# Where the low parts of the attention weights are computed: vector engine or GpSimd, in a three-branch attention kernel on Trainium2

## The chip, the cores and the metric

The kernel runs on one core of a Trainium2 chip, as one program and one launch. The metric is device microseconds from start to end. A core has five engines with queues of their own: TensorE (PE, with its weight loads listed apart as PEld), VectorE (DVE), ScalarE (ACT), GpSimd (POOL) and SyncE (SP), which here only issues DMAs. Each engine takes its instructions strictly in the order of its queue; waits between engines are semaphores.

## The reference

One layer of a hybrid decoder on a sequence of 512 rows with 1024 channels, all in float32. The input is RMS-normed and projected by one large matrix; three attention branches (A: block-sparse with blocks of 256; B: three dilated windows with dilation 1, 4 and 16; C: a sliding window of 128 with sinks) work on heads of 64; their outputs are gated, projected and merged. Cut to what matters:

```python
hn = rms_norm(x, ln_g[l])
proj = jnp.einsum('bsd,dc->bsc', hn, w_in[l])
(qa, ka, va, ga, qb, kb, vb, gb, qc, kc, vc, gc, gate_logits) = jnp.split(proj, SPLIT_POINTS, axis=-1)
...   # q and k of every head are RMS-normed: rms_norm(q.reshape(b, s, H, HEAD_DIM), g)
o_a = moba_attention(qa, ka, va, rel_bias_a)
o_b = dilated_attention(qb, kb, vb, rel_bias_b)
o_c = swa_sink_attention(qc, kc, vc, sinks[l], rel_bias_c)
branches = jnp.stack([o_a * jax.nn.silu(ga), o_b * jax.nn.silu(gb), o_c * jax.nn.silu(gc)], axis=2)
br = jnp.einsum('bsiw,iwd->bsid', branches, w_branch[l])
merged = jnp.sum(jax.nn.sigmoid(gate_logits) * br, axis=2)
x = x + jnp.einsum('bsd,de->bse', merged, w_out[l])
```

## The kernel before

**Split operands.** TensorE multiplies in the type fp32r, so every float32 operand is split in two: a high part `hi` (the value rounded to fp32r, a cast) and a low part `lo = value - hi` (a subtraction). A product is three matmuls: hi by hi, hi by lo, lo by hi. The weights come by DMA in tiles `w32` of 128x1024 floats (four buffers). For each, ScalarE casts `whi` (`split_hi`, L132), and one of two engines subtracts to get `wlo` (`split_lo`, L137); `whi` and `wlo` have six buffers each. The subtraction reads two operands from SBUF and writes one to SBUF.

**Who subtracts.** `load_w` (L148 to L167) counts the weight tiles of the whole kernel in `nw`. On L164 the tiles whose number is divisible by `every` go to GpSimd, the rest to the vector engine. The default of `every` is `LOEVERY`, 4 before the change. The very first call has `early=True` and alternates. The loads of the branch projections and of the output projection pass `every=1000`; the faster gate blocks have a loader of their own (`fast_weights`) whose subtractions are on the vector engine. None of these change.

**Stages.** The attention is done in ten units: A0, W0, R0, Z0, A1, W1, R1, Z1, C0, C1 (W, R and Z are branch B with dilation 1, 4 and 16; the digit is the half of the heads). A unit's weights are six tiles: four for q and k, two for v (C0 has four in all, C1 two). First a unit is projected (L492, L493 and L494 are the three matmuls, in four row blocks t = 0 to 3). For q and k each row block goes through a chain: ScalarE copies the result to `qn` (L504) and squares it (L506); the vector engine sums (`ss`, L508) and adds the epsilon (`rv`, L141); **GpSimd takes the power -1/2 (`rr`, L143)**; the vector engine multiplies (`qn`, L519); TensorE transposes (`tr`, L549); ScalarE and the vector engine make the high and low parts `qhi`, `khi`, `qlo`, `klo` (L559, L560). So `rr` and the weight subtractions of GpSimd share one queue. Then the unit's attention runs: scores on TensorE (`sc`; L652, L750), minimum and sum on the vector engine (L576), the exponential on ScalarE (L577), transposes (L672, L761), `pthi` on ScalarE and `ptlo` on the vector engine (L132 and L137 with other operands), and the weighted values (L565 to L567, L602). In a window of the code the projection matmuls of the next unit are put between the steps of this one's attention, to keep TensorE busy. After every Z unit branch B is merged: statistics are transposed (`trs` L953), permuted by three copies on ScalarE (`un`, L957) and transposed back (`trb`, L960).

After C1 come the raw gate columns and, from about 480 us on, the gate blocks and projections. Jobs 0, 1 and 2 (raw B, raw A and the first gate block) are loaded with `load_w`; these are what the code calls `n < PLAIN`.

**Order.** The engines' order is not written out by hand. The program is built in a context that schedules with a model of the times (`schedule_with_timeline_sim=True`), so when an instruction changes its engine, the order on all engines is worked out anew.

Of the kernel before, what the change touches and what calls it, by code (L numbers as in the profile page):

```python
# [20 lines left out]
KT = 8  # L21
# [7 lines left out]
UNITS = ("A0", "W0", "R0", "Z0", "A1", "W1", "R1", "Z1", "C0", "C1")  # L29
SPILL = [(k, h) for k in "ABC" for h in range(2) if UNITS.index(("Z" if k == "B" else k) + str(h)) < len(UNITS) - KEEP]  # L30
ORDER = "BAC"
LOEVERY = 4


RATION = {"A0": (52, 0.65), "W0": (52, 0.65), "W1": (52, 0.65), "C0": (8, 0.6), "C1": (0, 0.9)}
# [65 lines left out]
def body(tc, x, ln_g, w_in, qk_g, sinks, w_branch, w_out, rel_bias, c_ident, c_onehot, c_mask, c_expand, out):  # L101
# [9 lines left out]
    with top:  # L111
# [18 lines left out]
        def split_hi(dst, src, eng=A):  # L130
            if eng is A:
                A.copy(dst, src)  # L132
            else:
                eng.tensor_copy(dst, src)  # L134

        def split_lo(dst, src, hi, eng=V):
            eng.tensor_tensor(dst, src, hi.bitcast(F32), ALU.subtract)  # L137
# [9 lines left out]

        def load_w(pieces, kts, early=False, every=LOEVERY):  # L148


            ncol = sum(n for n, _ in pieces)
            per = 1024 // ncol
            his, los = [], []
            for k0 in range(0, kts, per):
                w = wp.tile([128, per, ncol], F32, name="w32", tag="w32", bufs=LBUFS)
                o = 0
                for n, src in pieces:
                    nc.sync.dma_start(w[:, :, o : o + n], src(k0, k0 + per))
                    o += n
                hi = wp.tile([128, per, ncol], F32R, name="whi", tag="whi")  # L160
                lo = wp.tile([128, per, ncol], F32R, name="wlo", tag="wlo")
                nw[0] += 1
                split_hi(hi, w, V if early and nw[0] % 2 else A)
                split_lo(lo, w, hi, G if nw[0] % (2 if early else every) == 0 else V)  # L164
                his.append(hi)
                los.append(lo)
            return (lambda k: his[k // per][:, k % per]), (lambda k: los[k // per][:, k % per])  # L167

        def win_piece(c, n):
            return (n, lambda k0, k1: win[:, k0:k1, c : c + n])  # L170
# [106 lines left out]
        def fast_weights(src):  # L277

            L = {}
            for i, k in ((0, 0), (1, 0), (1, 1), (0, 1)):
                L[i, k] = wp.tile([128, 4, 256], F32, name="w32", tag="w32", bufs=LBUFS)
                nc.sync.dma_start(L[i, k], src(i, k))
            sets = []

            def parts(w, eng):
                hi = wp.tile([128, 4, 256], F32R, name="whi", tag="whi")
                lo = wp.tile([128, 4, 256], F32R, name="wlo", tag="wlo")
                split_hi(hi, w)  # L290
                split_lo(lo, w, hi, eng)
                sets.append((hi, lo))

            sm = gp.tile([128, 4, 256], F32, name="sm", tag="sm", bufs=1)
            parts(L[0, 0], V)
            V.tensor_tensor(sm, L[1, 0], L[1, 1], ALU.add)
            parts(sm, V)
            V.tensor_tensor(sm, sm, L[0, 0], ALU.subtract)
            parts(sm, V)
            parts(L[0, 1], V)  # L300
            V.tensor_tensor(L[0, 0], L[0, 0], L[1, 0], ALU.subtract)
            parts(L[0, 0], V)
            parts(L[1, 1], V)
            V.tensor_tensor(sm, L[0, 1], sm, ALU.subtract)
            parts(sm, V)
            return sets
# [97 lines left out]
        def job_load(n):  # L404
            if n >= len(jobs):
                return None
            ty, u, v = jobs[n]
            if ty in ("raw", "gl"):
                c0 = v if ty == "raw" else GL + v * D + u * 512
                if n < PLAIN:  # L410
                    return load_w([win_piece(c0, 512)], KT)
                return fast_weights(lambda i, k: win[:, 4 * k : 4 * k + 4, c0 + 256 * i : c0 + 256 * i + 256])
            if ty == "br":
                return load_w([(512, lambda k0, k1: wbr[v, :, k0:k1, u * 512 : u * 512 + 512])], 4, every=1000)
            return load_w([(1024, lambda k0, k1: wou[:, k0:k1, :])], KT, every=1000)
# [7 lines left out]
        def raw_columns():  # L423
            jw[0] = job_load(0)
            for n in range(2):
                br = jobs[n][1]
                jw[n + 1] = job_load(n + 1)
                for hf in range(2):
                    raw = raw_tile(br, hf)
                    for p in range(2):  # L430
                        pj = ps.tile([128, 512], F32, name="pj", tag="pj")
                        yield from gate_cols(jw[n], (hf * 2 + p) * 128, pj)
                        A.copy(raw[:, p], pj)
# [598 lines left out]
        for n in range(2, len(jobs) - 1):  # L1032
            ty, dh, i = jobs[n]
            if n == PLAIN:
                xs = fast_x()
            w, wnext = wnext, job_load(n + 1)
            if ty == "raw":
                fast_cols(w, xs, [raw_tile(dh, hf) for hf in range(2)], keep)
# [92 lines left out]
```

## Time and profile before

| | |
|---|---|
| median of three runs | 805.29 us (805.21 to 806.34) |
| the profiled execution | 808.76 us |
| its span, first to last instruction | 807.0 us |
| TensorE busy | 783.0 us, 97% |
| vector engine busy | 515.6 us, 64% |
| ScalarE busy | 432.4 us, 54% |
| GpSimd busy | 128.2 us, 16% |
| mean granted TensorE clock | 0.987 of full |

The span is 1.76 us shorter than its execution's time. The profiled execution is 3.5 us longer than the median of the runs. Times of rows below are microseconds from the start of the span. "x2" in a row of the timeline means two instructions in a row, with their total time; the bracket is the engine's idle time before, and what ended it.

### The profile page before, as it was taken

How to read it: one execution, taken by the hardware profiler on the slowest of the kernel's cores; microseconds unless marked ns; L12 is line 12 of the kernel's file. 1: busy time of each engine (PE TensorE's matmuls, PEld its weight loads, DVE VectorE, ACT ScalarE, POOL GpSimd, SP SyncE). 2: the span in 40 equal slices, each digit the busy share in tenths (PEclk: the TensorE clock that was granted, in tenths of full speed). 3: DMA queues.
4: the chain of work that ended last, by engine and by line, in shares of the span. 5: the costliest groups of instructions: out<-in, count | busy, mean ns of one | idle time of the engine just before them, and what ended most of it. 6: DMA issues, size and time to landing. Idle time of an engine off the chain costs nothing.

```text
span 807.0 us, 12636 instructions
## 1 busy us (share of the span) xinstructions
PE 783.0 (97%) x4727; PEld 663.4 (82%) x4727; DVE 515.6 (64%) x1088; ACT 432.4 (54%) x938; POOL 128.2 (16%) x90
## 2 busy tenths in 40 slices
PE   7999999999998999999999899999999999999997
PEld 4887887788878777878887787788899999999886
DVE  6765664564554667346554486848889887987512
ACT  5534564666577356447775865766355244445300
POOL 5422211112310340122032042100000000000000
PEclk9999999999998999999999699999999999999999
DMA  9443343351331153414431221414143334436302
GB/s 280 126 150 85 103 121 102 106 168 35 105 111 27 52 157 79 142 46 147 131 105 33 80 65 42 154 54 137 46 157 123 90 102 131 131 101 201 117 1 104
DMA packets 67328, 85.72 MB, mean 106 GB/s; under 512 B 4899, under 2 KB 53155, under 8 KB 67268
## 3 DMA queue, kind: packets, MB, share of 16 engines
q1 hardware_dynamic: 67268, 84.93, 34.2%
q8 instruction: 37, 0.61, 0.3%
q14 instruction: 23, 0.19, 0.1%
HBM read 75.41 MB, written 9.50 MB: 105 GB/s over the span
## 4 chain that ended last, share of the span: by engine, by line
PE 88%; DVE 4%; ACT 4%; issue 2%; DMA 1%; POOL 0%; SPq 0%; DVEq 0%; ACTq 0%; POOLq 0%
PE pj L492 13%; PE pj L493 12%; PE pj L494 12%; PE fc L352 10%; PE acc L1090 5%; PE fsc L352 4%; PE po L602 3%; PE sc L652 3%; PE pj L272 2%; PE pj L274 2%; PE pj L273 2%; PE po L1060 2%; PE po L1061 2%; PE po L1062 2%; PE tr L672 2%; PE tr L549 2%
## 5 line engine op out<-in xcount | busy, mean ns | idle before, releaser
L492 PE MATMUL pj<-whi,xhi 128*128 128x512 f32 (+1 forms) x576 | 203.9, 354 | 2.0 <-DVE whi L134 0.9
L493 PE MATMUL pj<-wlo,xhi 128*128 128x512 f32 (+1 forms) x576 | 199.2, 346 | 0.0
L494 PE MATMUL pj<-whi,xlo 128*128 128x512 f32 (+1 forms) x576 | 198.1, 345 | 0.0
L132 ACT CAST whi<-w 128x1024 fp32r<-128x1024 f32 x108 | 112.8, 1050 | 77.5 <-PE fsc L352 18.7
L137 DVE TENSOR_TENSOR wlo<-w,whi 128x1024 fp32r<-128x1024 f32 x93 | 117.6, 1273 | 39.1 <-ACT whi L132 38.4
L492 PEld LDWEIGHTS pj<-whi,xhi 128*128 128x128 f32 x576 | 111.0, 193 | 18.6 <-ACT xhi L132 1.7
L493 PEld LDWEIGHTS pj<-wlo,xhi 128*128 128x128 f32 x576 | 111.1, 193 | 12.4 <-issue 0.8
L494 PEld LDWEIGHTS pj<-whi,xlo 128*128 128x128 f32 x576 | 111.0, 193 | 12.4 <-issue 0.5
L143 POOL TENSOR_TENSOR rr<-rv,mhalf 128x8 f32<-128x8 f32 (+2 forms) x40 | 65.7, 1644 | 218.3 <-DVE rv L141 199.0
L137 DVE TENSOR_TENSOR ptlo<-tr,pthi 128x128 fp32r<-128x128 f32 (+3 forms) x112 | 50.9, 458 | 30.6 <-ACT pthi L132 22.4
L132 ACT CAST pthi<-tr 128x128 fp32r<-128x128 f32 (+3 forms) x112 | 44.4, 400 | 39.9 <-PE tr L672 19.5
L137 POOL TENSOR_TENSOR wlo<-w,whi 128x1024 fp32r<-128x1024 f32 x17 | 41.1, 2419 | 98.5 <-ACT whi L132 98.5
L519 DVE TENSOR_TENSOR qn<-qn,rr 128x512 f32<-128x512 f32 (+1 forms) x36 | 30.9, 858 | 32.9 <-POOL rr L143 32.8
L576 DVE CUSTOM_DVE_ANT_0 lg<-sc,bt 128x128 f32<-128x128 f32 (+2 forms) x96 | 28.5, 335 | 24.6 <-PE sc L652 12.2
L508 DVE TENSOR_REDUCE ss<-sq 128x8 f32<-128x512 f32 (+2 forms) x40 | 25.7, 642 | 28.8 <-ACT sq L506 28.4
L577 ACT ACTIVATE lg<-lg,sm 128x128 f32<-128x128 f32 (+1 forms) x80 | 32.8, 411 | 14.0 <-DVE sm L576 13.7
L352 PE MATMUL fc<-xlo,whi 128*128 128x256 f32 x144 | 40.2, 279 | 0.0
L352 PE MATMUL fc<-xhi,wlo 128*128 128x256 f32 x144 | 40.2, 279 | 0.0
L352 PE MATMUL fc<-xhi,whi 128*128 128x256 f32 x144 | 40.2, 279 | 0.0
L272 PE MATMUL pj<-xhi,whi 128*128 128x512 f32 x96 | 39.2, 408 | 0.0
L504 ACT COPY qn<-pj 128x512 f32<-128x512 f32 (+1 forms) x36 | 20.6, 571 | 33.3 <-PE pj L494 33.3
L273 PE MATMUL pj<-xlo,whi 128*128 128x512 f32 x96 | 37.9, 395 | 0.0
(259 smaller groups left out, 1752.7 us busy)
## 6 DMA issues: line engine op xcount, KB each, us to landing
w<-in_w_in SPq DMA_DIRECT2D x54, 512.0 KB, 4.2
w<-in_w_in SPq DMA_DIRECT2D x72, 256.0 KB, 3.8
w<-in_w_branch SPq DMA_DIRECT2D x12, 512.0 KB, 3.5
vscr<-vn SPq DMA_DIRECT2D x16, 256.0 KB, 2.8
w<-in_w_out SPq DMA_DIRECT2D x8, 512.0 KB, 4.6
osp<-oraw SPq DMA_DIRECT2D x6, 512.0 KB, 4.2
oback<-osp SPq DMA_DIRECT2D x6, 512.0 KB, 3.6
xt<-in_x SPq DMA_DIRECT2D x4, 512.0 KB, 6.6
```

Of the source, the lines that this page charges most:

```text
L132: A.copy(dst, src)
L137: eng.tensor_tensor(dst, src, hi.bitcast(F32), ALU.subtract)
L143: G.tensor_tensor(r, v, mhalf[:, :n], ALU.pow)
L272: T.matmul(psum, a, xhi[:, k, :], start=(k == 0), stop=False)
L273: T.matmul(psum, a, xlo[:, k, :], start=False, stop=False)
L352: T.matmul(psum[:, c], w[:, k, cs], x_[:, k, :], start=(first and c == 0 and k == 0 and q == 0), stop=(c == 1 and k == 3 and q == 2), skip ...
L492: T.matmul(pj[:, :ncol], xh, whi(k), start=(k == 0), stop=False)
L493: T.matmul(pj[:, :ncol], xh, wlo(k), start=False, stop=False)
L494: T.matmul(pj[:, :ncol], xl, whi(k), start=False, stop=(k == KT - 1))
L519: V.tensor_tensor(q3[:, :nq], q3[:, :nq], r[:, :nq].unsqueeze(2).broadcast_to([128, nq, 64]), ALU.mult)
L577: last_exp[0] = A.activation(lg, lg, AF.Exp, bias=mcol, scale=-1.0, accum_out=lcol)
L1090: T.matmul(acc[t * 2 + e], part[k // 2][:, k % 2, tsl], wo[q](k)[:, es], start=(k == 0 and q == 0 and part is mhi), stop=(k == KT - 1 and ...
```

## The change

Two edits. `LOEVERY` goes from 4 to 1, so that all weight tiles loaded with the default go to GpSimd: in the attention all but two of the four tiles of the early call. And the three gate jobs loaded with `load_w` now pass `every=2`, so every second of their 12 tiles goes to GpSimd (before: every fourth).

```diff
-LOEVERY = 4
+LOEVERY = 1
...
                 if n < PLAIN:
-                    return load_w([win_piece(c0, 512)], KT)
+                    return load_w([win_piece(c0, 512)], KT, every=2)
```

Counted in the program, 41 of the 93 subtractions `wlo<-w32,whi` of the vector engine move: GpSimd has 58 of them after the change and 17 before, the vector engine 52 and 93. No other instruction is added or removed, but the schedule is worked out anew. In the rows below a number behind a name is that of the tile, the same in both programs.

**The end of unit Z1, vector engine.** Here (the rows at 440 to 446 us) the weight tiles 5108 to 5126 of raw B are split, between the softmax steps of the last Z unit. Before:

```order
L576 ISA sm_3443 128x1
L137 TENSOR_TENSOR wlo_5108<-w32_5105,whi_5107 128x1024
L137 TENSOR_TENSOR wlo_5120<-w32_5117,whi_5119 128x1024
L137 TENSOR_TENSOR wlo_5126<-w32_5123,whi_5125 128x1024
L576 ISA lg_4530,sm_3443<-sc_4517,bt_4518 128x128
L576 ISA sm_3443 128x1
L576 ISA lg_4530,sm_3443<-sc_4517,bt_4518 128x128
L576 ISA sm_3443 128x1
L137 TENSOR_TENSOR ptlo_98<-tr_4476,pthi_97 128x512
```

After:

```order
L516 TENSOR_TENSOR qn_4761<-qn_4761,rr6_4769 128x64 x2
L137 TENSOR_TENSOR wlo_5108<-w32_5105,whi_5107 128x1024
L137 TENSOR_TENSOR wlo_5120<-w32_5117,whi_5119 128x1024
L576 ISA lg_4530,sm_3443<-sc_4517,bt_4518 128x128
L576 ISA sm_3443 128x1
L576 ISA lg_4530,sm_3443<-sc_4517,bt_4518 128x128
L576 ISA sm_3443 128x1
L137 TENSOR_TENSOR ptlo_98<-tr_4476,pthi_97 128x512
```

One subtraction, wlo_5126, has left the queue ahead of `ptlo`; wlo_5120 is still there. On GpSimd wlo_5126 now stands directly behind wlo_5114.

**The end of unit Z0, vector engine.** Here stand the third row block's `qn` of unit A1 (with `rr8_2626`), eight softmax steps of Z0, and weight tiles of W1 (q and k). Before:

```order
L576 ISA lg_2305,sm_1253<-sc_2276,bt_2279 128x128
L576 ISA sm_1253 128x1
L519 TENSOR_TENSOR qn_2618<-qn_2618,rr8_2626 128x512
L137 TENSOR_TENSOR wlo_2805<-w32_2801,whi_2804 128x1024
L137 TENSOR_TENSOR wlo_2819<-w32_2815,whi_2818 128x1024
L137 TENSOR_TENSOR wlo_2826<-w32_2822,whi_2825 128x1024
L576 ISA lg_2352,sm_1253<-sc_2339,bt_2340 128x128
```

After:

```order
L508 TENSOR_REDUCE ss_2622<-sq_2620 128x8
L141 TENSOR_SCALAR rv8_2624<-ss_2622 128x8
L519 TENSOR_TENSOR qn_2618<-qn_2618,rr8_2626 128x512
L576 ISA lg_2289,sm_1253<-sc_2276,bt_2277 128x128
L576 ISA sm_1253 128x1
L576 ISA lg_2289,sm_1253<-sc_2276,bt_2277 128x128
L576 ISA sm_1253 128x1
L576 ISA lg_2289,sm_1253<-sc_2276,bt_2279 128x128
```

The three subtractions have left. `qn_2618` stood behind the eight softmax steps and stands ahead of them now.

**The merge of branch B after Z0, TensorE.** The transposes `trs_2402` feed the copies `un_2407` of ScalarE, for which `trb_2411` waits. Before:

```order
L953 MATMUL trs_2402<-idr_63,sl_1251 96x128 x4
L549 MATMUL tr_2542<-idr_63,qn_2526 128x128 x2
L494 MATMUL pj_2714<-whi_2271,xlo_65 128x256
L549 MATMUL tr_2583<-idr_63,qn_2572 128x128 x2
L492 MATMUL pj_2714<-whi_2271,xhi_64 128x256
L493 MATMUL pj_2714<-wlo_2272,xhi_64 128x256
L494 MATMUL pj_2714<-whi_2271,xlo_65 128x256
L960 MATMUL trb_2411<-idr_63,un_2407 128x96 x4
```

After, the last rows ahead of `trb_2411`:

```order
L494 MATMUL pj_2772<-whi_2265,xlo_65 128x256
L492 MATMUL pj_2772<-whi_2265,xhi_64 128x256
L493 MATMUL pj_2772<-wlo_2266,xhi_64 128x256
L494 MATMUL pj_2772<-whi_2265,xlo_65 128x256
L492 MATMUL pj_2772<-whi_2271,xhi_64 128x256
L493 MATMUL pj_2772<-wlo_2272,xhi_64 128x256
L494 MATMUL pj_2772<-whi_2271,xlo_65 128x256
L960 MATMUL trb_2411<-idr_63,un_2407 128x96 x4
```

Between `trs_2402` and `trb_2411` there were 4 projection matmuls and two pairs of transposes; now there are 39 projection matmuls and two such pairs.

**The projection of W0, GpSimd.** The powers are those of W0's last three row blocks, the weight tiles 1196 to 1230 are R0's. Before:

```order
L143 TENSOR_TENSOR rr8_739<-rv8_737,mhalf_67 128x8
L137 TENSOR_TENSOR wlo_1216<-w32_1212,whi_1215 128x1024
L143 TENSOR_TENSOR rr8_785<-rv8_783,mhalf_67 128x8
L143 TENSOR_TENSOR rr8_831<-rv8_829,mhalf_67 128x8
L810 MEMSET sl_2842 128x384
```

After:

```order
L143 TENSOR_TENSOR rr8_785<-rv8_783,mhalf_67 128x8
L137 TENSOR_TENSOR wlo_1196<-w32_1193,whi_1195 128x1024
L137 TENSOR_TENSOR wlo_1202<-w32_1199,whi_1201 128x1024
L137 TENSOR_TENSOR wlo_1209<-w32_1205,whi_1208 128x1024
L137 TENSOR_TENSOR wlo_1216<-w32_1212,whi_1215 128x1024
L143 TENSOR_TENSOR rr8_831<-rv8_829,mhalf_67 128x8
```

Four subtractions in a row now stand between the powers of the third and of the fourth row block, where there were none; the one before `rr8_785` has gone behind it. The same pattern, four subtractions in a row between a unit's third power and its fourth, stands in GpSimd's queue after the change in the chains of A0, R0, Z0, A1, R1 and Z1 too: seven times in all.

## Rows read from the trace of the kernel before

**Rows 1.** Page, part 1: busy us (share of the span) and instructions of each engine.

```profile
PE 783.0 (97%) x4727; PEld 663.4 (82%) x4727; DVE 515.6 (64%) x1088; ACT 432.4 (54%) x938; POOL 128.2 (16%) x90
```

**Rows 2.** Page, part 4: the chain that ended last, by engine.

```profile
PE 88%; DVE 4%; ACT 4%; issue 2%; DMA 1%; POOL 0%; SPq 0%; DVEq 0%; ACTq 0%; POOLq 0%
```

**Rows 3.** Page, part 5: groups, busy us, mean ns | idle before, releaser.

```profile
L137 DVE TENSOR_TENSOR wlo<-w,whi 128x1024 fp32r<-128x1024 f32 x93 | 117.6, 1273 | 39.1 <-ACT whi L132 38.4
...
L137 POOL TENSOR_TENSOR wlo<-w,whi 128x1024 fp32r<-128x1024 f32 x17 | 41.1, 2419 | 98.5 <-ACT whi L132 98.5
L519 DVE TENSOR_TENSOR qn<-qn,rr 128x512 f32<-128x512 f32 (+1 forms) x36 | 30.9, 858 | 32.9 <-POOL rr L143 32.8
```

**Rows 4.** Waits of PE: engine, line, waited for: us in total, times, longest.

```profile
PE po L566 <- DVE ptlo L137: 3.3, 5, 2.1
PE trb L960 <- ACT un L957: 2.7, 1, 2.7
...
PE tr L549 <- DVE qlo L560: 0.8, 2, 0.4
...
PE tr L672 <- DVE qlo L560: 0.7, 1, 0.7
PE tr L549 <- DVE klo L560: 0.6, 1, 0.6
```

**Rows 5.** Windows: length, busy us by engine, granted clock (PEclk), DMA share, GB/s.

```profile
252.90:256.20 3.30, 3.30 (x18) 3.30 (x17) 1.27 (x5) 3.16 (x5) 1.64 (x1) 0.50 0.26 76
447.40:461.00 13.60, 12.48 (x56) 10.67 (x55) 3.81 (x11) 12.87 (x32) 0.00 (x0) 0.50 0.20 78
```

**Rows 6.** Timeline, end of unit Z1: start, us, engine, operation, [idle <-releaser].

```profile
440.86 2.37 POOL L137 TENSOR_TENSOR wlo<-w,whi 128x1024 fp32r<-128x1024 f32 x1 [7.41 <-ACT whi L132]
441.76 3.69 DVE L137 TENSOR_TENSOR wlo<-w,whi 128x1024 fp32r<-128x1024 f32 x2 [1.83 <-ACT whi L132]
...
445.79 0.68 DVE L137 TENSOR_TENSOR ptlo<-tr,pthi 128x512 fp32r<-128x512 f32 x1
...
446.52 0.39 PE L566 MATMUL po<-ptlo,vhi 128*128 128x256 f32 x1 [2.12 <-DVE ptlo L137]
```

**Rows 7.** Timeline, end of unit Z0 and the merge of branch B.

```profile
227.03 0.69 DVE L519 TENSOR_TENSOR qn<-qn,rr 128x512 f32<-128x512 f32 x1
227.64 1.22 DVE L137 TENSOR_TENSOR wlo<-w,whi 128x1024 fp32r<-128x1024 f32 x1
231.57 3.67 DVE L137 TENSOR_TENSOR wlo<-w,whi 128x1024 fp32r<-128x1024 f32 x2 [2.71 <-ACT whi L132]
...
240.20 0.33 PE L761 MATMUL tr<-idr,lg 128*128 128x128 f32 x1 [0.82 <-ACT lg L577]
...
251.24 0.55 PE L960 MATMUL trb<-idr,un 96*128 96x96 f32 x4 [2.67 <-ACT un L957]
```

**Rows 8.** Timeline: vector-engine instructions beside a subtraction of GpSimd, two places.

```profile
80.70 2.20 DVE L141 TENSOR_SCALAR rv<-ss 128x8 f32<-128x8 f32 x1
...
413.64 2.41 POOL L137 TENSOR_TENSOR wlo<-w,whi 128x1024 fp32r<-128x1024 f32 x1
...
413.71 2.89 DVE L519 TENSOR_TENSOR qn<-qn,rr 128x512 f32<-128x512 f32 x1 [0.39 <-POOL rr L143]
```

**Rows 9.** Timeline, projection of W0: the last two powers and what follows.

```profile
83.04 3.24 POOL L143 TENSOR_TENSOR rr<-rv,mhalf 128x8 f32<-128x8 f32 x2 [0.17 <-DVE rv L141]
...
86.31 0.69 DVE L519 TENSOR_TENSOR qn<-qn,rr 128x512 f32<-128x512 f32 x1 [0.21 <-POOL rr L143]
...
89.35 0.83 PE L549 MATMUL tr<-idr,qn 128*128 128x128 f32 x4 [0.40 <-DVE qlo L560]
```

**Rows 10.** Timeline, attention of A1 with the projection of W1 (317 to 319 us).

```profile
317.18 1.21 DVE L137 TENSOR_TENSOR wlo<-w,whi 128x1024 fp32r<-128x1024 f32 x1
...
318.83 0.44 PE L549 MATMUL tr<-idr,qn 128*128 128x128 f32 x2 [0.35 <-DVE qlo L560]
```

**Rows 11.** Timeline, projection of Z1, last row block: its power and its transpose.

```profile
420.13 1.64 POOL L143 TENSOR_TENSOR rr<-rv,mhalf 128x8 f32<-128x8 f32 x1 [4.08 <-DVE rv L141]
...
427.08 0.38 PE L549 MATMUL tr<-idr,qn 128*128 128x128 f32 x2
```

**Rows 12.** Page, part 6: DMA issues, count, KB each, us to landing.

```profile
w<-in_w_in SPq DMA_DIRECT2D x72, 256.0 KB, 3.8
```

## The prediction

> **What bounds the kernel now.** I read the busy shares first: TensorE is busy for 783.0 of 807.0 us, the vector engine for 515.6, GpSimd for 128.2 [rows 1]. The chain of work that ended last is TensorE for 88%, vector engine 4%, ScalarE 4%, GpSimd 0% [rows 2]. So a faster vector engine saves time only where TensorE stands and waits for it. TensorE's idle time is 807.0 - 783.0 = 24 us, and the list of its waits says for whom: 3.3 us for `ptlo`, 2.7 for the copies `un`, and a row of waits of 0.6 to 0.8 each for `qlo` and `klo` [rows 4]. To this come stretches with the granted clock at 0.50, which is 1.2 GHz. They follow such waits: 252.9 to 256.2 us behind the wait for `un`, and 447.4 to 461.0 behind the wait of 2.1 us for `ptlo` [rows 5 to 7]. A matmul of the first stretch takes 3.30 / 17 = 0.19 to 0.21 us where the full clock takes about half, so the two stretches cost at most 1.7 and 6.8 us. What the change can gain lies in these waits and stretches, not in the 50 us that it takes off the vector engine.
>
> **What moves.** 41 subtractions leave the vector engine, at 1.22 us where nothing disturbs them (mean 1.273): 41 x 1.22 = 50 us. GpSimd takes 2.419 us for one [rows 3], so it gains 41 x 2.42 = 99 us, 128 to 227, still 28% of the span. Both totals lie beside TensorE's work. If all of the difference of 1.15 us lay on the path, it would be +47 us; it doesn't, since the chain that ended last has nothing of GpSimd. What counts is where a burst of them stands ahead of something TensorE needs.
>
> The Trainium skill speaks against the move: its GPSIMD Engine Reference, section 4.1 (Engine selection), sends elementwise work with two inputs to VectorE and calls GpSimd about twice as slow. The trace agrees, 2419 to 1273 ns. By that rule alone the sum would be the +47 us; it holds for an engine whose time counts, which GpSimd's here is not.
>
> **What GpSimd's subtraction does to the vector engine.** The trace shows a second cost. A vector instruction whose operands all lie in SBUF, issued while GpSimd subtracts, ends only behind it: L519 at 413.71 took 2.89 us, beside a subtraction of GpSimd from 413.64 for 2.41, where others take 0.69; a tiny `rv` took 2.20 [rows 8]. The subtractions of the vector engine itself are held too: the pair at 441.76 took 3.69 where 2 x 1.22 = 2.44 is usual, beside GpSimd's from 440.86 to 443.23 [rows 6], and the pair at 231.57 took 3.67 [rows 7]. So each L519 or `rv` that meets a burst loses some 2.0 to 2.2 us. The held subtractions become fewer, the held L519 and `rv` more.
>
> **Part by part.** Times are those of the rows of before.
>
> *End of Z1.* wlo_5126, the second of the pair at 441.76, leaves the queue ahead of `ptlo` at 445.79, for which TensorE waited 2.12 us until 446.52 [rows 6]. wlo_5120 stays, and stays held. `ptlo` comes 1.2 us sooner, other inputs allowing: **-1.1**. If two subtractions of GpSimd in a row hold the vector engine for both, it is up to +2.4 - 1.2 = +1.2 instead. No row shows two in a row; I take the gain, since in both held pairs the vector engine went on as soon as the first one ended.
>
> *End of Z0 and the merge.* The wait of 2.67 us before `trb` at 251.24 [rows 7] has 35 more projection matmuls ahead of it, of about 0.12 us each: 35 x 0.12 = 4.2 us of cover, more than the wait, so it goes, less a rest: **-2.4**. With it may go the stretch at half clock: **-1.7**. These matmuls stood elsewhere before, so TensorE has less to do ahead of them. There, `qn_2618` now stands before the eight softmax steps instead of behind them, and it can meet wlo_2805 on GpSimd, which follows `rr8_2626` directly: a hold of 2.2 us on the softmax, whose results TensorE already waited for (0.82 at 240.20). Three subtractions that stood at 227.64 and 231.57, 1.22 + 3.67 = 4.9 us, are no longer in the way of the next softmax steps. I take **+1.7** for waits that grow there, between -1.5 (nothing is held; the 4.9 us help) and +4 (two holds). Sum of the place: -2.4, between -5.6 and +1.6.
>
> *Attention of A1 and like places.* The subtraction at 317.18 is followed by `qlo`, for which TensorE waited 0.35 us at 318.83 and then ran a slower transpose, 0.44 [rows 10]: it leaves, **-0.5**. Of the other waits for `qlo` and `klo`, 0.8 + 0.7 + 0.6 in all [rows 4] with this one inside, some go with it: **-0.5**, between 0 and -1.5.
>
> *The powers behind bursts.* Seven times four subtractions, 4 x 2.42 = 9.7 us, stand between the third `rr` of a unit and the fourth. In W0's projection the two powers ended at 83.04 + 3.24 = 86.28, L519 followed at 86.31, and TensorE's transpose came at 89.35, behind a short wait for `qlo` [rows 9]. After the change the burst starts behind the third power. That came as late as 83.04 because its `rv` was held [rows 8] behind subtractions that leave; I put its end between 76.5 and 79.2, an estimate from the row block's copy that feeds it. Then the burst ends between 86.2 and 88.9, the fourth power 1.64 later, L519 0.69 later, at 88.5 to 91.2; TensorE reached the transpose at 89.35 - 0.40 = 88.95. That is a wait of 0 to 2.3 us: **+1.1**. In Z1's projection the fourth power stood at 420.13 to 421.77 and its transpose at 427.08 [rows 11]; four subtractions behind the third power, which ended about 413.7 (GpSimd's next starts at 413.64 [rows 8]), end at 423.3, so the power slips by some 4 us and its L519 ends at 426.4: 0.7 us to spare. A1's chain is alike. A0's I put at +0.3. For those three **+0.8**, between 0 and +3. For the other three units I take nothing: their chains have what two holds cost, by the same counting, to spare.
>
> *Loads and buffers.* A weight tile's buffer is read until its subtraction ends, 1.2 us later than before and more within a burst. A tile lands 3.8 us after issue [rows 12], and the tiles are loaded a unit ahead: nothing; up to +1 if the SyncE queue stands behind one at a stage's start.
>
> *The first gate block.* Six instead of three of the 12 tiles on GpSimd; in Z1's end they are counted above. Behind 480 us there is nothing of GpSimd to collide with: nothing.
>
> **Sum.** -1.1 - 2.4 - 0.5 - 0.5 + 1.1 + 0.8 = -2.6 us. Against the profiled execution, 808.76, it is 806.2; that execution was 3.5 us above the median 805.29, so for the median I say **802.7**. Since the whole order is worked out anew, each place can move by some tenths in either direction; with the bounds above the forecast's own range is 798 to 806.
>
> **Rivals.**
> 1. *The bursts hold the chains* (slower). An `rv` or L519 of the fourth row block comes while the burst runs and is held 2.0 to 2.2 us, and the power behind it is late by 4 us already. Where 0.7 us are to spare a second hold shows as 1.3 to 1.5 us on TensorE, where nothing is to spare as 2.0. It decides from the point where L519 ends behind TensorE's reaching the transpose. Four of the seven bursts at 2.0: 802.7 + 8.0 = 810.7; two: 806.7. For it: rows 8 and 11. Against: the four subtractions are not always ready in a row, as each waits for its cast on ScalarE (98.5 us of GpSimd's idle time were spent so [rows 3]). Beside it, the GPSIMD Engine Reference of the Trainium skill, section 1 (Specifications), says that GpSimd shares its SBUF interfaces with VectorE and contends with its instructions that have two SBUF inputs; by that rule L519 and the low parts are held, and the trace agrees for L519, 2.89 for 0.69 us.
> 2. *Nothing in sum* (the same). TensorE is busy for 97%, the waits that go come back in other places as the same matmuls fill them: 805.3 +- 1.6.
> 3. *The long stretch at half clock goes as well* (faster). If the wait at the end of Z1 falls from 2.1 to about 1 us and the clock doesn't fall behind it, up to 6.8 us [rows 5] come back: 802.7 - 6.8 = 795.9. Against: ScalarE was busy 12.87 of these 13.6 us and TensorE waited there in many short pieces, which stay.
>
> That the change does nothing of what it says is excluded by the order: 41 subtractions stand on the other engine.
>
> **How the numbers follow.** A difference of 0.2%, 1.6 us, is about what a measurement of this kernel can tell. Forecast 0.42 (all faster); rival 3 0.12; rival 2 0.20; rival 1 0.26. So faster 0.54, same 0.20, slower 0.26. The range, 796.0 to 810.0, reaches to the middle of rival 1 and to rival 3 and leaves out some 0.1 at each end.
>
> **What would show it.** Right: the vector engine's busy time falls by 40 to 55 us and GpSimd's rises by about 99; TensorE's wait for `un` near 250 us is under 0.5; its wait for `ptlo` near 446 is about 1; L519 rows of 2.4 to 2.9 us become more than the few of now, but few are followed by a wait of TensorE at L549. Wrong: TensorE's waits at L549 or for L519's results of 1 to 2 us at the ends of projections (rival 1); the sum of TensorE's idle time unchanged at 24 us (rival 2); a stretch at half clock that is gone, or a new one (rival 3). My forecast falls if the reordering moved waits to places that I didn't go through, or if the vector engine is held for a whole burst.

## The result, and the profile after

The changed kernel takes 800.55 us (median of 4 runs, 799.89 to 801.07), the kernel before 805.82 beside it (4 runs, 805.21 to 807.13): a ratio of 0.9940, 95% interval 0.9927 to 0.9954. That is faster by 0.6%, or 5.3 us. Run once more, with e9 to e11, it was 0.9939 (0.9926 to 0.9953). The forecast was 2.6 us, to 802.7.

The profiled execution has a span of 799.3 us, 7.7 less than that of before. Busy shares and groups of the changed kernel:

```profile
PE 776.3 (97%) x4727; PEld 657.8 (82%) x4727; DVE 476.6 (60%) x1047; ACT 433.9 (54%) x938; POOL 224.1 (28%) x131
...
L137 POOL TENSOR_TENSOR wlo<-w,whi 128x1024 fp32r<-128x1024 f32 x58 | 140.7, 2442 | 113.8 <-ACT whi L132 99.9
...
L137 DVE TENSOR_TENSOR wlo<-w,whi 128x1024 fp32r<-128x1024 f32 x52 | 66.1, 1280 | 20.9 <-ACT whi L132 20.8
...
L519 DVE TENSOR_TENSOR qn<-qn,rr 128x512 f32<-128x512 f32 (+1 forms) x36 | 35.8, 996 | 23.2 <-POOL rr L143 23.0
```

Beside [rows 1, 3] the vector engine is busy 39.0 us less, GpSimd 95.9 us more. The mean of L519 went from 858 to 996 ns: more of them are held, which means that they have to wait for a subtraction of GpSimd to end. Waits of TensorE of the changed kernel:

```profile
PE po L566 <- DVE ptlo L137: 2.0, 4, 1.0
PE tr L761 <- ACT lg L577: 1.8, 3, 1.1
...
PE tr L549 <- DVE klo L560: 1.1, 1, 1.1
PE tr L672 <- DVE qlo L560: 0.9, 1, 0.9
PE tr L672 <- ACT lg L577: 0.8, 1, 0.8
PE tr L549 <- DVE qn L519: 0.7, 1, 0.7
```

The wait for `un` of [rows 4] is gone; that for `ptlo` fell from 3.3 to 2.0; waits for `lg` at L672 and for L519's result are new, that for `lg` at L761 is longer (0.8 before). TensorE's idle time fell only from 24.0 to 23.0 us. The rest of the profiled gain, 6.7 us, is in its busy time, of which a part is the clock. Span and mean granted clock of before, and then of the changed kernel:

```profile
core 0: 807.0 us, clock 0.987
...
core 0: 799.3 us, clock 0.991
```

A microsecond at the lower level, 1.2 GHz (a granted clock of 0.50), loses half at most, and (1 - 0.987) x 807 = 10.5 us, (1 - 0.991) x 799 = 7.2 us: up to 3.3 us of the 7.7 in this pair of executions are clock. The gain of the medians is not: when the two were run once more, the executions of the changed kernel had mean clocks of 0.991 to 0.995, those of the kernel before 0.992 to 0.996.

**Where the time went, by stage.** Instructions stand in another order in the two programs, so I lined them up by TensorE's work: every matmul of the program's order is given its pace (0.233 us for 512 columns, 0.117 for 256, 0.109 for 128; half for the scores' pairs), these are added up, and the trace tells when each sum was reached. The table gives the change against before in us, by stretches of before. Columns are single profiled executions, the changed kernel twice (ch, again), then the experiments by number (below; e5, which does more work, is left out). The execution of before is 3 us above its median, so gains look that much larger here; those of e6, e7, e8 and e9 were the fastest of their runs.

```
before, us        ch  again    e1    e2    e3    e4    e6    e7    e8    e9   e10   e11
  4.2- 32.8      1.1   -0.7   0.0  -0.3  -0.7  -1.5  -1.7  -1.2  -1.9  -0.5  -2.0   0.0
 32.8-142.9     -1.2   -0.3   0.1  -0.4   0.2  -2.2  -0.1  -1.4  -1.2  -1.5  -1.2  -1.3
142.9-168.0     -1.9   -1.9  -1.9   0.0  -0.5  -0.3   0.0  -1.9  -1.9  -1.9   0.0  -1.9
210.8-263.5     -3.2   -4.4  -2.8  -0.4  -1.8  -0.3  -3.2  -1.9  -4.4  -4.9   0.0  -2.9
263.5-354.5      0.3    0.3   0.3   0.1  -0.8   0.2  -1.1   0.2  -0.5   3.1  -0.1  -0.5
354.5-379.1     -2.0   -2.0  -2.0   0.0  -0.5   0.0   0.0  -2.0  -1.9  -2.0   0.0  -2.0
422.0-446.9     -1.1   -1.1   0.1  -1.1  -1.2  -1.1   0.0  -1.1  -1.1  -1.1   0.0  -1.1
446.9-474.3     -1.3   -1.2  -1.1   0.1  -1.8   0.2  -1.8  -1.4  -1.9  -1.3  -2.0  -1.4
474.3-580.0      1.7    1.7   1.2   2.3   0.2  -0.9  -0.4   0.3   0.4   1.7   1.2  -0.9
```

The stretches left out change by under 0.5, and behind 580 us nothing changes. The first row moves by 2 us even between two executions of the same kernel; the rows with -1.9, -2.0 and -1.1 repeat to a tenth.

Some of the other rows move with the clock. This is the time that each execution spent at 1.2 GHz in three of the stretches, the first column being the kernel before:

```
us at 1.2 GHz  before    ch  again    e1    e2    e3    e4    e6    e7    e8    e9   e10   e11
210.8-263.5       6.8   3.4    0.0   3.4   6.8   6.8   6.8   3.4   6.8   0.0   0.0   6.8   3.4
446.9-474.3      13.6   6.8    6.8   6.8  10.2   0.0  10.2   3.4   3.4   0.0   3.4   3.4   3.4
474.3-580.0       0.0   3.4    3.4   3.4   3.4   0.0   0.0   0.0   0.0   0.0   3.4   3.4   0.0
```

At half a microsecond for each, up to 1.7 us of the changed kernel's -3.2 at the end of Z0 and up to 3.4 of the second execution's -4.4 are clock. Without this, all columns lie between -1.0 and -1.9 there, but for e2, e4 and e10 with 0 to -0.4. Behind 474 us the columns with a stretch at 1.2 GHz have +1.2 to +2.3, the others -0.9 to +0.4. Between 446.9 and 474.3 us, 10 to 14 us less at 1.2 GHz are worth only 1.3 to 2.0 us. In the rows with -1.9, -2.0 and -1.1 no execution was at 1.2 GHz.

### The profile page after: what moved, and what is told of

Same layout as the page of the kernel before. It is cut to its first block, busy times and chain, and to the rows that moved or that the text cites. A ratio compares the mean times of both kernels' runs of the same rounds, so it can differ in the third digit from the quotient of the medians.

```text
span 799.3 us, 12655 instructions
## 1 busy us (share of the span) xinstructions
PE 776.3 (97%) x4727; PEld 657.8 (82%) x4727; DVE 476.6 (60%) x1047; ACT 433.9 (54%) x938; POOL 224.1 (28%) x131
## 4 chain that ended last, share of the span: by engine, by line
PE 85%; ACT 5%; DVE 3%; DMA 2%; POOL 2%; issue 2%; SPq 0%; DVEq 0%; ACTq 0%; POOLq 0%
PE pj L492 11%; PE pj L494 11%; PE pj L493 11%; PE fc L352 11%; PE acc L1090 6%; PE fsc L352 4%; PE po L602 3%; PE pj L272 3%; PE pj L274 3%; PE pj L273 3%; DMA w<-in_w_in 2%; PE sc L652 2%; PE po L1060 2%; PE po L1061 2%; PE po L1062 2%; PE tr L672 2%
## 5 line engine op out<-in xcount | busy, mean ns | idle before, releaser
L492 PE MATMUL pj<-whi,xhi 128*128 128x512 f32 (+1 forms) x576 | 201.7, 350 | 2.1 <-DVE whi L134 1.2
L493 PE MATMUL pj<-wlo,xhi 128*128 128x512 f32 (+1 forms) x576 | 197.1, 342 | 0.0
L137 POOL TENSOR_TENSOR wlo<-w,whi 128x1024 fp32r<-128x1024 f32 x58 | 140.7, 2442 | 113.8 <-ACT whi L132 99.9
L492 PEld LDWEIGHTS pj<-whi,xhi 128*128 128x128 f32 x576 | 109.4, 190 | 17.5 <-ACT xhi L132 2.0
L494 PEld LDWEIGHTS pj<-whi,xlo 128*128 128x128 f32 x576 | 109.2, 190 | 13.8 <-DVE xlo L137 1.0
L143 POOL TENSOR_TENSOR rr<-rv,mhalf 128x8 f32<-128x8 f32 (+2 forms) x40 | 63.8, 1596 | 164.5 <-DVE rv L141 157.8
L137 DVE TENSOR_TENSOR wlo<-w,whi 128x1024 fp32r<-128x1024 f32 x52 | 66.1, 1280 | 20.9 <-ACT whi L132 20.8
L508 DVE TENSOR_REDUCE ss<-sq 128x8 f32<-128x512 f32 (+2 forms) x40 | 25.7, 643 | 53.6 <-ACT sq L506 53.1
L519 DVE TENSOR_TENSOR qn<-qn,rr 128x512 f32<-128x512 f32 (+1 forms) x36 | 35.8, 996 | 23.2 <-POOL rr L143 23.0
L577 ACT ACTIVATE lg<-lg,sm 128x128 f32<-128x128 f32 (+1 forms) x80 | 32.8, 411 | 10.9 <-DVE sm L576 10.5
L274 PE MATMUL pj<-xhi,wlo 128*128 128x512 f32 x96 | 38.2, 398 | 0.0
```

The lines of the kernel that those rows point to most:

```text
L143: G.tensor_tensor(r, v, mhalf[:, :n], ALU.pow)
L274: T.matmul(psum, wlo(k)[:, c : c + 128], xhi[:, k, :], start=False, stop=(k == KT - 1))
L492: T.matmul(pj[:, :ncol], xh, whi(k), start=(k == 0), stop=False)
L493: T.matmul(pj[:, :ncol], xh, wlo(k), start=False, stop=False)
L494: T.matmul(pj[:, :ncol], xl, whi(k), start=False, stop=(k == KT - 1))
L519: V.tensor_tensor(q3[:, :nq], q3[:, :nq], r[:, :nq].unsqueeze(2).broadcast_to([128, nq, 64]), ALU.mult)
```

## The experiments

**Theories.** *Places*: the gain is made where a subtraction left the vector engine's queue ahead of something that TensorE needs soon; it is local to the tiles moved. *Order*: any change of engine makes the order new, and the gain is an accident of that. *Holds*: what counts is how long GpSimd holds the vector engine. *Bursts* (rival 1 of the prediction; a burst is a row of subtractions of GpSimd): the powers behind four subtractions come too late.

### The two edits apart

e1, the units' tiles alone:

```diff
-LOEVERY = 4
+LOEVERY = 1
...
-                    return load_w([win_piece(c0, 512)], KT)
+                    return load_w([win_piece(c0, 512)], KT, every=4)
```

> Only the units' tiles move to GpSimd; the first three gate jobs keep every fourth tile (55 subtractions on GpSimd). Places theory (the gain is made where a subtraction left the vector engine's queue ahead of something TensorE needs): the end of Z1 is where this edit is felt, wlo_5126 stays ahead of ptlo there, so about 2 us of the gain of 5.3 are missing: 802 to 803 us, TensorE's wait for ptlo at the end of Z1 about 2.1 us again. Order theory (the gain is an accident of the new order): any time from 799 to 806, no link to that wait. If the gate edit does nothing: 800.5.

Measured: 802.14 us (7 runs), ratio 0.9943 (0.9920 to 0.9965). The wait for `ptlo` is back, as the timeline of e1 shows:

```profile
435.54 3.69 DVE L137 TENSOR_TENSOR wlo<-w,whi 128x1024 fp32r<-128x1024 f32 x2 [1.82 <-ACT whi L132]
...
440.31 0.39 PE L566 MATMUL po<-ptlo,vhi 128*128 128x256 f32 x1 [2.12 <-DVE ptlo L137]
```

This is the picture of [rows 6]: 3.69 us for the pair, a wait of 2.12. The table has 0.1 here and -1.1 for the changed kernel. The place is as the places theory says, but in the time no difference from the changed kernel (0.9940) can be told.

e2, the gate jobs alone:

```diff
-                    return load_w([win_piece(c0, 512)], KT)
+                    return load_w([win_piece(c0, 512)], KT, every=2)
```

> Only the three gate jobs change, every second of their tiles; the units keep every fourth (20 subtractions on GpSimd). Places theory: only the end of Z1 and behind it gains, 1 to 2 us: 804 to 805 us, the wait for the copies un after Z0 stays at 2.7 us. If the gate edit carries the change: about 801.

Measured: 806.42 us (12 runs), ratio 1.0009 (0.9992 to 1.0026): nothing, where the places theory expected 804 to 805. The 1.1 us at the end of Z1 are there (row 422 to 447), and are given back behind 474 us, +2.3, where this execution has a stretch at 1.2 GHz. The gain of the change is that of the first edit.

### How many, or which

e3, `LOEVERY = 2` and the gate jobs as changed; e4, none but the early call's two:

```diff
-LOEVERY = 1
+LOEVERY = 1000
...
-                    return load_w([win_piece(c0, 512)], KT, every=2)
+                    return load_w([win_piece(c0, 512)], KT, every=1000)
```

> Every second tile of the units on GpSimd, every second of the gate jobs (33 subtractions on GpSimd). Places theory: part of the places gain; about half, 802 to 804 us; the wait for un after Z0 stays, since the order ahead of its transposes is as before. If the number of subtractions on the vector engine were what counts, 41 x share: 16 of 41 moved would give 2.1 of 5.3 us, 803.7.

Measured: 803.13 us (12 runs), ratio 0.9960 (0.9942 to 0.9978), as expected; the wait for `un` stays at 2.7.

> All subtractions but two of the early call on the vector engine (2 on GpSimd). Places theory: more stands ahead of TensorE's needs than before, fewer holds: slower than before by 2 to 6 us, 808 to 812. If the holds of the vector engine by GpSimd (18 us of stretch before) cost more than the subtractions themselves: faster than before, 800 to 804. Order theory: either.

Measured: 801.62 us (10 runs), ratio 0.9952 (0.9935 to 0.9969). **This was a miss**: with all subtractions back on the vector engine the kernel is faster than before too, by about as much as with all on GpSimd. So neither direction is good by itself; every fourth, as before, was the worst of these four (ratios with 2, 17, 33 and 58 subtractions on GpSimd: 0.9952, 1, 0.9960, 0.9940). What speaks for the holds as the second cost are the groups of e4:

```profile
L137 DVE TENSOR_TENSOR wlo<-w,whi 128x1024 fp32r<-128x1024 f32 x108 | 132.6, 1237 | 41.2 <-ACT whi L132 40.3
...
L519 DVE TENSOR_TENSOR qn<-qn,rr 128x512 f32<-128x512 f32 (+1 forms) x36 | 24.8, 688 | 23.6 <-POOL rr L143 23.6
```

L519's mean is 688 ns, with hardly a hold left, where it was 858 before and 996 in the changed kernel. And the table says where: e4 gains 2.2 us between 33 and 143, 1.1 at the end of Z1 and 0.9 behind 474 (e10 and e11 below take these places one by one), and next to nothing at 143 to 168 and 354 to 379, where the changed kernel gains 1.9 and 2.0.

### Is it local?

If so, units can be chosen. For each of these, `loads` passes an `every` by unit:

```diff
                 kind, hf, gi = unit
+                ev = LOEVERY if kind + str(hf) in ("Z0", "W1", "Z1") else 1000
...
-                return [load_w(qk, KT, early), load_w(vv, KT)]
+                return [load_w(qk, KT, early, ev), load_w(vv, KT, every=ev)]
```

That is e8, made from the changed kernel, with the gate jobs at every second. e7: all units but A0, W0 and R0. e9: Z0 and Z1 alone. e11: as e8, with the gate jobs at `every=1000`. Made from the kernel before: e6, W1's tiles all on GpSimd, the others every fourth; e10, A0, W0 and R0 on the vector engine, the others every fourth.

> The kernel before, with only W1's six tiles all on GpSimd (they are split at the end of Z0; 21 subtractions on GpSimd). Places theory: the gain of the changed kernel between 200 and 265 us, 3.2 us, comes alone: 802 to 803 us; the wait for un goes, the rest of the trace stays as before. If the gain at the merge comes from the whole order and not from these tiles: 805.4, un still 2.7 us.

Measured: 803.02 us (12 runs), ratio 0.9964 (0.9945 to 0.9983). The time is as expected, the way is not. Waits of TensorE of e6:

```profile
PE po L566 <- DVE ptlo L137: 3.3, 5, 2.1
PE trb L961 <- ACT un L958: 2.7, 1, 2.7
```

The wait for `un` stayed at 2.7 (its line is one lower in this file). W1's tiles are not what removes it. Of the 3.2 us that this execution gains at the end of Z0, up to 1.7 are clock. What is left, 1.5, is no less than in the runs without that wait: its going is paid back by other waits there.

> The changed kernel, with the tiles of A0, W0 and R0 on the vector engine (44 subtractions on GpSimd). The run with none on GpSimd had gained 3.5 us by 143 us where the changed one had gained 0.2; behind that the changed one gains and the other doesn't. If the two costs (holds of the vector engine early, subtractions ahead of attention steps later) are local: 796 to 798. If the order decides: anything between 799 and 806.

Measured: 799.14 us (6 runs), ratio 0.9928 (0.9903 to 0.9953). This is **a miss** for places, which said 796 to 798, and in the time no difference from the changed kernel can be told. The table has -1.4 from 33 to 143 us, where the two executions of the changed kernel have -1.2 and -0.3: what the early subtractions cost in the changed kernel is within what two executions differ by.

> All units' tiles on the vector engine but those of Z0, W1 and Z1, which are all on GpSimd (26 with the early call's and the gate jobs' every second). These are the places where the changed kernel gained: 1.9 us in the attention of W0 and of W1 each, 3.2 at the end of Z0. If the costs are local: 794 to 798. If the order decides: anything between 799 and 806.

Measured: 796.40 us (4 runs), ratio 0.9893 (0.9863 to 0.9923): faster than both kernels, within the 794 to 798 that places gave. Its span and clock, and a window over the end of Z0 of the changed kernel and then of e8:

```profile
core 0: 792.3 us, clock 1.000
```

```profile
225.00:265.00 40.00, 37.22 (x244) 31.55 (x241) 19.79 (x66) 29.47 (x78) 16.20 (x7) 0.96 0.32 95
```

```profile
225.00:265.00 40.00, 37.08 (x253) 31.01 (x252) 19.61 (x83) 30.51 (x81) 14.79 (x8) 1.00 0.33 96
```

TensorE stands idle as long in both windows (2.8 and 2.9 us), but in e8 its clock stayed whole, here and over the whole span. The profiled execution of e8 was the fastest of its four (794.06 of 794.06 to 797.66), so part of its lead in the table is the clock of that execution. The clock is most of its lead over the changed kernel too: the mean clocks of its four executions were 0.995 to 1.000, those of the changed kernel's nine 0.991 to 0.995. Each kernel has one execution at 0.995, of 797.66 and 797.95 us. Whether e8's order is what keeps the clock up is not shown.

> As the run with Z0, W1 and Z1 on GpSimd, but W1's tiles on the vector engine (20 subtractions on GpSimd). Places theory: the attention of W0 and of W1 keep their 1.9 us each, the end of Z0 loses the gain of the queue: W1's three or four subtractions of 1.22 us stand ahead of the softmax again; but the order now has a long row of projection matmuls ahead of trb, so the wait for un should be gone: 797 to 799. If the gain at the end of Z0 needs W1's tiles away from the vector engine: un's wait is replaced by waits for ptlo or lg of about the same, 799 to 801.

Measured: 801.24 us (5 runs), ratio 0.9961 (0.9946 to 0.9975), outside both expectations. The attention of W0 and of W1 keeps its 1.9 and 2.0. At the end of Z0 it gains 4.9 (up to 3.4 of it clock), `un` is waited for only 0.2: projection matmuls stand ahead of `trb` without W1's tiles on GpSimd too. But 3.1 us are lost behind it. W1's tiles stand on the vector engine there, but so they do in e4, which loses 0.2, so these tiles alone do not make the loss; what does stays open, and the new order is not excluded. The longest wait there, from e9's timeline:

```profile
301.02 0.66 PE L672 MATMUL tr<-idr,lg 128*128 128x128 f32 x4 [1.72 <-ACT lg L577]
```

> The kernel before, with only the tiles of A0, W0 and R0 taken off GpSimd (14 subtractions on GpSimd). It isolates what the early subtractions of GpSimd cost. If the holds of the vector engine cost TensorE time there (three early rows of 2.2 to 2.9 us): gains of 0.5 to 2 us between 33 and 143 us as in the run with none on GpSimd, 803.5 to 804.5; the rest as before. If the early gain was only a matter of how the start fell in a single execution: 805.4.

Measured: 803.53 us (11 runs), ratio 0.9984 (0.9971 to 0.9997): 1.3 us, by the interval 0.2 to 2.3, as expected. So much the subtractions of GpSimd in the first three units cost the kernel before, and the row 33 to 143 shows it, -1.2. In before an `rv` took 2.20 [rows 8], being held; here no L519 or `rv` between 70 and 90 us takes more than 0.69. Lined up by TensorE's work, 0.9 of the 1.2 us are gained between 85 and 90 us of before, right behind that `rv`, and e4, e7 and e8 gain the same 0.9 there.

> As the run with Z0, W1 and Z1 on GpSimd, but the three gate jobs wholly on the vector engine (20 subtractions on GpSimd). At the end of Z1 the pair of wlo then stands with one or two more on the vector engine ahead of ptlo, but none of them is held: between 796 (the hold was the cost, nothing lost) and 798.5 (the queue was the cost, 1.1 us and a stretch at half clock lost).

Measured: 795.67 us (4 runs), ratio 0.9891 (0.9878 to 0.9905), the best, not to be told from e8. The row 422 to 447 has -1.1 here as in e8: it takes both, GpSimd's subtraction that holds the first of the pair and the second of the pair behind it, to make TensorE wait 2.1 us. Taking away either gives the 1.1.

Behind 474 us e11 and e4, the two without a gate tile on GpSimd, gain 0.9. In before, a multiply `qb` (L519) is held there at 476.03 us, and TensorE then waits 0.91; e11 has neither. From the timelines of before and then of e11:

```profile
475.97 2.39 POOL L137 TENSOR_TENSOR wlo<-w,whi 128x1024 fp32r<-128x1024 f32 x1
476.03 2.62 DVE L519 TENSOR_TENSOR qb<-qb,rr 128x256 f32<-128x256 f32 x1 [0.74 <-POOL rr L143]
...
481.82 0.51 PE L475 MATMUL tr<-revr,qs 128*128 128x128 f32 x4 [0.91 <-DVE klo L560]
```

```profile
464.85 0.40 DVE L519 TENSOR_TENSOR qb<-qb,rr 128x256 f32<-128x256 f32 x1
```

> The changed kernel once more, on the chip of these runs, to set the others beside it: ratio to before 0.994, 800 to 801 us; the half-clock stretches may fall differently in this execution, the waits of TensorE don't.

Measured: 800.19 us (5 runs), ratio 0.9939 (0.9926 to 0.9953).

So as the whole explanation the order theory falls: the stretches 143 to 168 and 354 to 379 gain 1.9 to 2.0 in all seven runs of the table with Z0's and Z1's tiles wholly on GpSimd, and 0 to 0.5 in the five without. It is not excluded everywhere: at the end of Z0 the new order of the matmuls is part of the change, and the 3.1 us that e9 loses are not explained. The first of the two stretches, timeline of before and then of the changed kernel:

```profile
155.13 1.23 DVE L137 TENSOR_TENSOR wlo<-w,whi 128x1024 fp32r<-128x1024 f32 x1 [1.24 <-ACT whi L132]
156.28 0.75 DVE L137 TENSOR_TENSOR ptlo<-tr,pthi 128x256 fp32r<-128x256 f32 x2
156.94 1.22 DVE L137 TENSOR_TENSOR wlo<-w,whi 128x1024 fp32r<-128x1024 f32 x1
158.08 0.42 DVE L576 CUSTOM_DVE_ANT_0 lg<-sc,bt 128x256 f32<-128x256 f32 x1
...
159.11 0.40 PE L492 MATMUL pj<-whi,xhi 128*128 128x256 f32 x1 [0.44 <-ACT qn L504]
```

```profile
154.05 4.75 POOL L137 TENSOR_TENSOR wlo<-w,whi 128x1024 fp32r<-128x1024 f32 x2 [1.76 <-ACT whi L132]
```

Before, subtractions stood between the steps of W0's attention on the vector engine, each ahead of a `ptlo` or a softmax; now GpSimd does them beside, and those steps have an operand in PSUM and are not held. The same 166 matmuls of TensorE, in windows of before and then of the changed kernel, columns as in [rows 5]:

```profile
142.90:168.00 25.10, 24.16 (x166) 19.96 (x165) 15.55 (x42) 15.76 (x43) 5.67 (x3) 1.00 0.39 122
```

```profile
142.70:165.90 23.20, 23.03 (x166) 19.44 (x165) 12.65 (x39) 16.93 (x46) 12.81 (x6) 1.00 0.40 123
```

TensorE's idle time falls from 0.94 to 0.17 us, its busy time from 24.16 to 23.03 at the same clock. So over half of the 1.9 us stood in what the profile counts as busy time, where no list of waits has it.

### The bursts

e5: the changed kernel, each subtraction of GpSimd twice:

```diff
-                split_lo(lo, w, hi, G if nw[0] % (2 if early else every) == 0 else V)
+                e = G if nw[0] % (2 if early else every) == 0 else V
+                split_lo(lo, w, hi, e)
+                if e is G:
+                    split_lo(lo, w, hi, e)
```

> The changed kernel, with each subtraction of GpSimd done twice in a row (116 instead of 58 for the same tiles; GpSimd +140 us, about 365 us, still under half of the span). If the bursts have room, as the sum of the busy times says: under 804. If the bursts of four ahead of the fourth power have used up nearly all room (0.7 us left in Z1's projection by the prediction), each of the seven bursts is longer by 9.7 us and TensorE has to wait for most of it: 7 x 5 to 9 us, 835 to 865, with waits at L549 for L519's results.

Measured: 821.79 us (4 runs), ratio 1.0203 (1.0173 to 1.0233), between both expectations. The profiled execution has a span of 818.0 us, 18.7 more than the changed kernel's, and TensorE is idle for 36.2 us instead of 23.0. Waits of TensorE of e5 (lines are 3 lower), and then W0's projection, the last two powers on GpSimd and the two waits for what hangs on them:

```profile
PE tr L552 <- DVE qn L522: 5.0, 2, 3.7
...
PE tr L552 <- ACT kf L558: 2.8, 2, 1.4
PE tr L478 <- DVE klo L563: 2.7, 1, 2.7
PE trb L963 <- ACT un L960: 2.7, 1, 2.7
```

```profile
72.19 13.66 POOL L137 TENSOR_TENSOR wlo<-w,whi 128x1024 fp32r<-128x1024 f32 x5
85.82 1.63 POOL L143 TENSOR_TENSOR rr<-rv,mhalf 128x8 f32<-128x8 f32 x1
...
89.76 2.08 POOL L143 TENSOR_TENSOR rr<-rv,mhalf 128x8 f32<-128x8 f32 x1
...
90.49 0.63 PE L552 MATMUL tr<-idr,qn 128*128 128x128 f32 x4 [1.29 <-DVE qn L522]
94.84 1.09 PE L552 MATMUL tr<-idr,qn 128*128 128x128 f32 x4 [3.72 <-DVE qn L522]
```

The power waits behind the burst and TensorE behind the power: 5.0 us, all in W0's projection. In Z1's, which has a burst of six, no such wait came. So rival 1's mechanism exists, but of the 13.2 us of idle time that came on top these waits make 5.0, against 0.7 in the changed kernel; the rest is in other waits, which the new order brought along (`un` is waited for again). In the changed kernel the bursts have room but for those 0.7 us, and GpSimd's share of busy time (28%) tells nothing of that.

## Why the prediction was right, point by point

- *End of Z1, -1.1*: -1.1. The timeline of the changed kernel answers to [rows 6]:

```profile
433.84 5.67 POOL L137 TENSOR_TENSOR wlo<-w,whi 128x1024 fp32r<-128x1024 f32 x2 [4.84 <-ACT whi L132]
434.74 2.55 DVE L137 TENSOR_TENSOR wlo<-w,whi 128x1024 fp32r<-128x1024 f32 x1 [1.83 <-ACT whi L132]
...
437.63 0.68 DVE L137 TENSOR_TENSOR ptlo<-tr,pthi 128x512 fp32r<-128x512 f32 x1
...
438.37 0.39 PE L566 MATMUL po<-ptlo,vhi 128*128 128x256 f32 x1 [0.98 <-DVE ptlo L137]
```

  wlo_5120 is held as before, 2.55 us; `ptlo` follows after two softmax steps, and the wait is 0.98. The feared hold over two subtractions did not come: the vector engine went in between, and GpSimd's second took 5.67 - 2.37 = 3.3 us.
- *End of Z0 and the merge, -2.4*: -3.2, and -4.4 in the second execution. The parts held: `trb` follows without a wait; `qn_2618` met wlo_2805 (2.87 us at 224.94), and waits for `lg` grew from 0.8 to 1.6. The kernel before has two stretches at half clock here, 3.4 us each, of which the prediction saw one; one is left in the changed kernel, none in its second execution. With 2.7 for `un` and 1.7 for each stretch that went, the waits that grew come to +1.2 and +1.7, as priced. But e3 and e6 gain as much here without the clock, and in them `un` is still waited for: that this wait goes is worth nothing by itself.
- *Attention of A1 and other waits, -0.5 and -0.5*: the stretch 264 to 355 rose by 0.3, with a new wait of 0.8 for `lg` at L672. In sum this term did not come.
- *The powers behind bursts, +1.1 for W0's projection and +0.8 for three others*: in W0 the wait came, from the timeline of the changed kernel:

```profile
75.43 1.64 POOL L143 TENSOR_TENSOR rr<-rv,mhalf 128x8 f32<-128x8 f32 x1 [4.32 <-DVE rv L141]
77.03 9.94 POOL L137 TENSOR_TENSOR wlo<-w,whi 128x1024 fp32r<-128x1024 f32 x4
86.90 1.66 POOL L143 TENSOR_TENSOR rr<-rv,mhalf 128x8 f32<-128x8 f32 x1
...
89.34 0.66 PE L549 MATMUL tr<-idr,qn 128*128 128x128 f32 x4 [0.72 <-DVE qn L519]
```

  It was 0.72 instead of 1.1, but not in sum a loss: between 85 and 90 us of before, where the hold of `rv` had cost 0.9 us too (e10), TensorE lost 0.4 us more than before, and it gained 0.7 between 75 and 80. The row 33 to 143 has -1.2, and -0.3 in the second execution. A0's and the other chains showed no wait at L549 for L519's result, so the +0.8 did not come.
- *The other three units, nothing*: **this was the step that failed**. In R0's and R1's own chains nothing was lost, but I had costed only the powers there. That Z0's and Z1's tiles leave the attention of W0 and W1 gives -1.9 and -2.0, which is not in the sum: TensorE's listed waits in the first of the two were only two of 0.4 us, and I had taken the list of waits (with the stretches at half clock) for all that could be gained.
- *Behind 480 us, nothing*: +1.7 behind 474 us in both executions, with a stretch at half clock at 474.6 to 478.0 us that the kernel before didn't have. And there was something of GpSimd to collide with: the subtraction at 475.97 us of before holds `qb` (e11). Windows of the changed kernel, columns as in [rows 5]:

```profile
440.60:447.40 6.80, 6.31 (x29) 5.19 (x28) 2.10 (x4) 6.16 (x15) 0.00 (x0) 0.50 0.38 143
474.60:478.00 3.40, 3.40 (x13) 2.92 (x13) 2.02 (x6) 1.67 (x6) 2.56 (x2) 0.51 0.00 0
```

- *The sum*: the places that the prediction went through were to give -2.6 and gave, by the table, -1.1 - 3.2 + 0.3 - 1.2 = -5.2; the others, which it put at nothing, +1.1 at the start, -1.9, -2.0, -1.3 and +1.7, together -2.4. These -7.6 are against an execution of before that was 3 us above its median; in the medians it is -5.3. So the direction came out, the end of Z1 and the merge for the stated reasons, but the size was half of what was measured: the costs of the bursts, +1.9, did not come, and the attention of W0 and W1 was missing. What was left out has both signs (-5.2 and +2.8 in this pair); that it cancels in part, so that the total missed by no more than half, is luck.
- *The signs*: the vector engine's busy time fell by 39.0 us, just under the 40 to 55 given. TensorE's idle time stayed at 23.0 of 24.0 us, which was to be a sign of rival 2 (nothing in sum), and yet the kernel got faster: idle time was the wrong thing to watch, since a good part of the gain is in what the profile counts as busy.
- *The hold itself* was put too widely, as that of every instruction with its operands in SBUF: the sums `ss` are not held (see below).
- *Rival 3*: the long stretch at half clock [rows 5] shrank from 13.6 us to 6.8 in the changed kernel (the first of the two windows above), and was absent in the profiled executions of e3 and e8. Its price of 6.8 us was too high: those two have -1.8 and -1.9 in that row. What makes the clock fall is not settled by these runs: at the end of Z0 it fell in one execution of the changed kernel and not in the other, with the same order.

## What to carry to other kernels

An engine's busy share says little on either side of such a move: look at what stands directly behind the moved instruction in both queues, and whether TensorE needs it within a few microseconds. Choose by place, not by count: a fixed fraction (every fourth) paid both costs here, while all tiles of three units on GpSimd and those of the other seven on the vector engine gained 1.1%, against 0.6%, though most of that lead is a higher granted clock. Where TensorE's idle time is small, line up the traces by work done: the list of waits had 0.8 us in a stretch that gained 1.9.

## What the runs showed of the hardware

- A multiply, a subtraction, an `rv` or a cast of the vector engine with all operands in SBUF that meets a subtraction of GpSimd ends only behind it, be it as small as an `rv` (0.17 us became 2.05 at 44.24 us in the changed kernel) or a cast of 128x16 (0.17 became 1.91 at 504.06). The row sums `ss` (L508) also have their operands in SBUF and took their usual 0.69 us in all seven places of the changed kernel where they met one. With an operand in PSUM (`ptlo`, `lg`, `qlo`) instructions took their usual time too.
- The hold is passed on in turns. In a row of two subtractions of GpSimd a waiting vector instruction goes in between, and then GpSimd waits. From the changed kernel, with a row sum during the second:

```profile
38.70 5.21 POOL L137 TENSOR_TENSOR wlo<-w,whi 128x1024 fp32r<-128x1024 f32 x2
38.77 2.88 DVE L519 TENSOR_TENSOR qn<-qn,rr 128x512 f32<-128x512 f32 x1
...
42.86 0.69 DVE L508 TENSOR_REDUCE ss<-sq 128x8 f32<-128x512 f32 x1 [0.51 <-ACT sq L506]
```

  The first took 2.40 us, to 41.10; L519 ended at 41.65, behind the first and not behind both; the second ran from 41.06 to 43.91 and took 2.85.
- The mean granted clock was 0.987 in the kernel before and 1.000 in one execution of e8, at most 10.5 us of loss against none: at this size of change, what the clock does can be as large as what the engines do. But time at 1.2 GHz need not cost half of it: 13.6 us of it behind the end of Z1 cost about 2.
